# mLSTM gates projected ahead of the HGRN core, and a PSUM bank of its own for the last stream's second norm broadcast

## The chip, the cores and the metric

The kernel runs on one core of a Trainium2 chip. The metric is the device time of one execution in microseconds (us). The core has five engines that matter here: TensorE (PE) for matrix products and transposes, VectorE (DVE), ScalarE (ACT), GpSimd (POOL), and SyncE (SP), which issues most of the DMAs. Each works through its own instructions in program order and waits at semaphores for the others. Products land in PSUM, in banks of 128 partitions by 512 fp32 values; all other tiles lie in SBUF.

## What is computed

Two layers of a trunk over 256 latent tokens and 256 context tokens, model width 1024, batch 1, in fp32. Each layer is a half-step SwiGLU FFN, a mixing of three parallel branches (windowed attention, mLSTM, HGRN2) on one combined projection, and a second half-step FFN. Every one of these sub-layers is wrapped in norms and in a modulation by the condition:

```python
def ada_pre(x, mod, j, g):
    return rms_norm(x, g) * (1.0 + mod[..., 3 * j + 1, :]) + mod[..., 3 * j, :]
def ada_post(x, y, mod, j, g, w):
    return x + w * mod[..., 3 * j + 2, :] * rms_norm(y, g)
def macaron_ffn(x, mod, j, g_pre, g_post, w1, w3, w2):
    h = ada_pre(x, mod, j, g_pre)
    y = (jax.nn.silu(h @ w1) * (h @ w3)) @ w2
    return ada_post(x, y, mod, j, g_post, 0.5)
```

The mLSTM has per token, head (4) and direction (2) an input gate `ml_i` and a log forget gate, `log_sigmoid(m_f + ml_f_bias)`. Their running sums and running maxima along the tokens give the decay between any two tokens and the stabiliser m. The HGRN2 has its own gates, queries and inputs (`h_f`, `h_q`, `h_i`) and does not use those of the mLSTM. Context tokens take part in both layers, but in layer 1 nothing of theirs is needed behind the mixing.

## The kernel before

**Layout.** Activations lie transposed: 128 channels on the partitions, the tokens along the free axis, context stream CS in columns 0 to 255, latent stream XS in 256 to 511. XT is the residual, in eight chunks d of 128 channels. A matrix product keeps fp32 precision by splitting both operands into a rounded high part and the low rest: `mm3` (L255 to L257) does high x high, high x low and low x high into one bank. Weights come in units of 512 rows by 256 columns: one DMA, one cast on ScalarE (`wh`, L238), one subtraction on VectorE (`wl`, L239), 128x1024 each. Input h is split likewise: `Pre.scaled` (VectorE, L389) multiplies a chunk of XT by the norm's broadcast row, ScalarE makes the high half (L397), VectorE the low half (L398).

**Stages.** Layer 0: FFN, mixing, FFN; layer 1: FFN, mixing (latents only behind it), FFN. The five borders that this document calls ends 1 to 5 are: FFN to mixing of layer 0 (around 420 to 446 us of the span), mixing to FFN (1050), FFN of layer 0 to FFN of layer 1 (1440), FFN to mixing of layer 1 (1833), mixing to last FFN (2220). At each of them the end of one stage and the norm ahead of the next are fused in `Post.steps`, stream after stream: first the lead stream (CS), then the last stream (XS). At end 5 there is only XS.

**`Post.steps`.** The stage's sums of squares arrive as columns of a bank. VectorE makes y1, the inverse root for the norm behind the stage (`rsqrt_cols`, L360 to L369, nine operations on 128x2 values), from it by algebra the mean square of the new residual (L512 to L518), and y2, the inverse root for the next norm (the same nine operations). `row_bcast` (L374) turns y1 and then y2 into rows r and r2 by two products each with the identity. VectorE multiplies the eight chunks of the stage's output by r (L530), POOL adds each to XT (L531), and then `Pre.chunk` makes h from XT and r2, chunk by chunk, and the next stage's first products follow. r and r2 share one bank:

```python
                rr = mx()
                r, r2 = rr[:, 0:256], rr[:, 256:512]
```

Three banks rotate in `mx`; a write into a bank waits until its readers are done. The steps are interleaved with the products of the stage by generators (`Pending`, `passes`): while PE works on the lead stream's first products, the last stream's steps run. At end 5 the transposes of XT for the output (L681) also stand in PE's order there.

**Mixing.** `mix` projects HF (the HGRN's forget gates, `passes`), HQ (`proj`, products in L255 to L257) and HI (`proj_tok`, L767 to L769: tokens on the partitions, 24 products of 256 columns to a group, three rotating banks, each group copied out by ScalarE, L770). Then comes the HGRN core (`hgrn`), and behind it the gates of the mLSTM: a DMA of the 16 gate columns on SP (L981), POOL places them in a zeroed 128x1024 tile (L983, L987), ScalarE and VectorE split it (`split_to`, L773, L774), 24 products of 512 columns give the gate values of all tokens (L992 to L994), and a chain follows: Abs, Exp, Ln on ScalarE (L999 to L1001), on VectorE log f (L1002, L1003), three scans for the running sum, cr = i - sum, three scans for the running maximum (L1008 to L1013), the split of cr into crs (cast L773 on ScalarE), lf, and exp(-lf) on ScalarE (L1018, L1019). The projections MQ/MK and MV follow in the code; eight transposes of 64x64 (L1028 running maximum, L1029 exp(-lf)) and two copies put the columns where the heads read them (`mcol`). Each head (`mlstm`) makes decay matrices by products with crs (L1062 to L1065) and Exp on ScalarE (L1071, L1077), multiplies them with q k (L1082 to L1090), normalises, transposes (L1112) and multiplies with v.

**Order.** A scheduler places every engine's instructions from the code; `tc.issue_after(e)` keeps an instruction behind another. So an engine's order is not that of the code, and can be read from the built program only.

Of the kernel before, what the change touches and what calls it, by code (L numbers as in the profile page):

```python
# [10 lines left out]
F32 = mybir.dt.float32  # L11
# [63 lines left out]
def body(tc, I, out, dbg=None):  # L75
    nc = tc.nc
    with tc.tile_pool(name="cst", bufs=1) as cst, \
# [341 lines left out]
        class Post:  # L419
# [82 lines left out]
            def steps(self, st, pre, rest=None):  # L502
# [16 lines left out]
                after = yield  # L519
                rr = mx()  # L520
                r, r2 = rr[:, 0:256], rr[:, 256:512]
# [302 lines left out]
        def mix(l, h, post, need_c, pre):  # L824
# [22 lines left out]
            for b0 in range(2):  # L847
                for u in range(2):
                    us[u] += unit(Win[512 * b0:512 * b0 + 512, OFF_HF + 256 * u:OFF_HF + 256 * u + 256], 4)
                part_end()  # L850
            ps = four()
# [12 lines left out]
            proj(Win, OFF_HQ, 1, h, a, b, cb_hq)  # L864
            proj_tok(Win, OFF_HI, h, HV)

# [111 lines left out]


            graw = tmb((128, 8, 16))  # L980
            nc.sync.dma_start(graw, Win[:, OFF_GATE:OFF_GATE + 16].rearrange("(k p) c -> p k c", p=128))  # L981
            gz, gwh, gwl = slab(shape=(128, 8, 128)), slab(F32R, (128, 8, 128)), slab(F32R, (128, 8, 128))
            G.memset(gz, 0.0)  # L983
            for w in range(2):
                for d in range(2):
                    c0 = 64 * w + 32 * d
                    G.tensor_copy(gz[:, :, c0:c0 + 4], graw[:, :, 8 * w + 4 * d:8 * w + 4 * d + 4])  # L987
            split_to((gwh, gwl), gz)
            gps = bx()
            for k in range(KD):  # L990
                mm(gps, gwh[:, k], h[k][:, 0, :], start=k == 0, stop=False)
                mm(gps, gwh[:, k], h[k][:, 1, :], start=False, stop=False)  # L992
                mm(gps, gwl[:, k], h[k][:, 0, :], start=False, stop=k == KD - 1)
            ip, fp = gps[0:64], gps[64:128]  # L994
# [454 lines left out]
```

## Time and profile before

| | us |
|---|---|
| median of 3 runs | 2432.51 |
| lowest and highest run | 2429.64 and 2435.65 |
| the profiled execution, device time | 2432.19 |
| the profiled execution, span of the trace | 2430.4 |
| PE busy in it | 2366.1 |
| VectorE, ScalarE, POOL busy | 1479.6, 975.5, 240.5 |

The profile comes from one execution. Its page gives busy times, the chain that ended last and the costliest groups of instructions. The trace behind it answers by line, by wait, by window and as a timeline; times there count from the start of the span. In a timeline's row a bracket tells how long the engine was idle ahead of it and what released it. "PEclk" is the clock granted to TensorE as a share of its full 2.4 GHz.

### The profile page before, as it was taken

How to read it: one execution, taken by the hardware profiler on the slowest of the kernel's cores; microseconds unless marked ns; L12 is line 12 of the kernel's file. 1: busy time of each engine (PE TensorE's matmuls, PEld its weight loads, DVE VectorE, ACT ScalarE, POOL GpSimd, SP SyncE). 2: the span in 40 equal slices, each digit the busy share in tenths (PEclk: the TensorE clock that was granted, in tenths of full speed). 3: DMA queues.
4: the chain of work that ended last, by engine and by line, in shares of the span. 5: the costliest groups of instructions: out<-in, count | busy, mean ns of one | idle time of the engine just before them, and what ended most of it. 6: DMA issues, size and time to landing. Idle time of an engine off the chain costs nothing.

```text
span 2430.4 us, 34706 instructions
## 1 busy us (share of the span) xinstructions
PE 2366.1 (97%) x13770; PEld 2004.5 (82%) x13770; DVE 1479.6 (61%) x2677; ACT 975.5 (40%) x1597; POOL 240.5 (10%) x233
## 2 busy tenths in 40 slices
PE   8999999998999999999999999999999989998998
PEld 6877778887887788887778898778799889797998
DVE  5687466655644643767946366874546667656554
ACT  3322332433843732433223332223334374754543
POOL 2000022100000112310002120000221000023000
PEclk9999999999999999999999999999999999998999
DMA  7656343311122033345543325563323125254664
GB/s 262 204 188 199 99 150 101 97 41 36 53 78 87 27 97 94 96 137 194 189 139 100 109 80 197 192 190 106 112 87 89 44 70 145 82 157 120 186 186 135
DMA packets 267270, 301.00 MB, mean 124 GB/s; under 512 B 11709, under 2 KB 233206, under 8 KB 267108
## 3 DMA queue, kind: packets, MB, share of 16 engines
q1 hardware_dynamic: 266448, 298.04, 39.2%
q8 instruction: 108, 1.77, 0.3%
q0 software_dynamic: 512, 0.68, 0.2%
q14 instruction: 54, 0.44, 0.1%
q10 hardware_dynamic: 148, 0.06, 0.0%
HBM read 297.70 MB, written 1.05 MB: 123 GB/s over the span
## 4 chain that ended last, share of the span: by engine, by line
PE 90%; DVE 5%; ACT 3%; issue 1%; DMA 1%; POOL 0%; SPq 0%; DVEq 0%; ACTq 0%; POOLq 0%
PE a L255 24%; PE a L256 24%; PE a L257 24%; PE a L768 1%; PE a L767 1%; PE a L769 1%; PE x L374 1%; PE x L883 1%; PE x L320 1%; PE b L1240 1%; PE x L1300 1%; PE x L1273 1%; PE b L256 1%; PE b L257 1%; PE x L1122 1%
## 5 line engine op out<-in xcount | busy, mean ns | idle before, releaser
L255 PE MATMUL a<-s,wh 128*128 128x512 f32 (+1 forms) x3266 | 1142.3, 351 | 9.1 <-ACT s L397 8.7
L256 PE MATMUL a<-s,wh 128*128 128x512 f32 (+1 forms) x3266 | 1139.6, 349 | 2.2 <-DVE s L398 1.8
L257 PE MATMUL a<-s,wl 128*128 128x512 f32 (+1 forms) x3266 | 1138.2, 349 | 0.0
L239 DVE TENSOR_TENSOR wl<-raw,wh 128x1024 fp32r<-128x1024 f32 (+1 forms) x414 | 515.8, 1256 | 466.5 <-ACT wh L238 461.7
L255 PEld LDWEIGHTS a<-s,wh 128*128 128x128 f32 x3266 | 616.6, 189 | 110.5 <-ACT s L397 10.3
L256 PEld LDWEIGHTS a<-s,wh 128*128 128x128 f32 x3266 | 618.6, 189 | 89.3 <-issue 4.1
L257 PEld LDWEIGHTS a<-s,wl 128*128 128x128 f32 x3266 | 618.3, 189 | 87.0 <-DVE s L615 2.5
L238 ACT CAST wh<-raw 128x1024 fp32r<-128x1024 f32 (+1 forms) x418 | 431.6, 1036 | 608.0 <-PE a L256 422.4
L311 DVE SCALAR_TENSOR_TENSOR s<-s,sc,s 128x512 f32<-128x512 f32 x448 | 306.6, 757 | 0.0
L415 POOL TENSOR_TENSOR s<-s,t 128x512 f32<-128x512 f32 (+1 forms) x35 | 52.3, 1495 | 1074.9 <-ACT s L411 1072.7
L612 DVE TENSOR_TENSOR u<-u,a 128x512 f32<-128x512 f32 (+1 forms) x84 | 51.7, 618 | 101.0 <-PE a L257 98.5
L614 ACT CAST s<-u 128x512 fp32r<-128x512 f32 (+1 forms) x88 | 48.9, 567 | 143.9 <-DVE u L612 126.1
L611 ACT ACTIVATE u<-a 128x512 f32<-128x512 f32 (+1 forms) x88 | 47.4, 542 | 144.4 <-PE a L257 144.4
L767 PE MATMUL a<-wh,s 128*128 128x256 f32 x256 | 74.8, 292 | 7.8 <-ACT s L770 7.3
L397 ACT ACTIVATE s<-t,mod 128x256 fp32r<-128x256 f32 x88 | 38.6, 500 | 94.7 <-DVE t L389 94.7
L1173 POOL TENSOR_TENSOR s<-s,u 128x512 f32<-128x512 f32 (+1 forms) x32 | 35.8, 1119 | 399.0 <-ACT wh L238 253.0
L768 PE MATMUL a<-wl,s 128*128 128x256 f32 x256 | 74.7, 292 | 0.3 <-DVE wl L239 0.3
L769 PE MATMUL a<-wh,s 128*128 128x256 f32 x256 | 74.5, 291 | 0.0
L531 POOL TENSOR_TENSOR XT<-XT,s 128x256 f32<-128x256 f32 x72 | 56.6, 826 | 132.7 <-DVE s L530 58.3
L615 DVE TENSOR_TENSOR s<-u,s 128x512 fp32r<-128x512 f32 (+1 forms) x88 | 53.3, 619 | 15.7 <-ACT s L614 15.5
L767 PEld LDWEIGHTS a<-wh,s 128*128 128x128 f32 x256 | 49.8, 194 | 10.4 <-ACT s L770 9.9
L461 POOL TENSOR_TENSOR s<-s,u 128x512 f32<-128x512 f32 (+1 forms) x29 | 36.9, 1271 | 209.7 <-DVE u L457 199.7
(346 smaller groups left out, 2363.8 us busy)
## 6 DMA issues: line engine op xcount, KB each, us to landing
raw<-in_ffn_w_dram SPq DMA_DIRECT2D x256, 512.0 KB, 3.8
s<-in_w_ada_dram SPq DMA_DIRECT2D x144, 512.0 KB, 6.1
raw<-in_w_in_dram SPq DMA_DIRECT2D x112, 512.0 KB, 3.7
raw<-in_w_out_dram SPq DMA_DIRECT2D x16, 512.0 KB, 3.4
raw<-in_ffn_w_dram SPq DMA_DIRECT2D x16, 256.0 KB, 2.6
raw<-in_w_branch_hg_dram SPq DMA_DIRECT2D x8, 512.0 KB, 3.4
raw<-in_w_branch_ml_dram SPq DMA_DIRECT2D x8, 512.0 KB, 3.4
raw<-in_w_branch_att_dram SPq DMA_DIRECT2D x8, 512.0 KB, 4.1
```

The costliest lines, as they stand in the source:

```text
L238: S.copy(hi[:, :n], raw[:, :n])
L239: (eng or V).tensor_tensor(lo[:, :n], raw[:, :n], hi[:, :n].bitcast(F32), op=ALU.subtract)
L255: mm(ps, hi, h[i][:, 0, a:b], start=first and i == 0, stop=False)
L256: mm(ps, hi, h[i][:, 1, a:b], start=False, stop=False)
L257: end = mm(ps, lo, h[i][:, 0, a:b], start=False, stop=last and i == n - 1)
L311: V.scalar_tensor_tensor(t[:, s], w, c, t[:, s], op0=ALU.mult, op1=ALU.add)
L415: eng.tensor_tensor(dst[:, a:b], dst[:, a:b], q[:, a:b], op=ALU.add)
L531: post_x.append(G.tensor_tensor(xt, xt, yt, op=ALU.add).ins)
L615: V.tensor_tensor(gt[:, 1, a:b], t[:, a:b], gt[:, 0, a:b].bitcast(F32), op=ALU.subtract)
L767: mm(ps, h[k][:, 0, tk], hi, start=k == 0, stop=False)
L768: mm(ps, h[k][:, 0, tk], lo, start=False, stop=False)
L769: mm(ps, h[k][:, 1, tk], hi, start=False, stop=k == KD - 1)
```

## The change

There are two parts. In `mix` the gates move ahead of HGRN: their DMA, the placing on POOL and the split directly behind the weights of HF, the 24 products and the chain behind HQ's projection, the transposes and `mcol` behind HI's projection. In `Post.steps` the last stream's r2 gets a bank of its own; its multiplies and adds are issued four ahead of the second broadcast and two each ahead of chunks 1 and 2; the lead stream's are issued behind its second broadcast; and all multiplies are kept behind the end of y2's chain. The lines of `mix` that are only moved stand once in the diff below; behind the change the lines L530, L531, L767 to L770, L773, L774, L681 have the numbers L533, L534, L782 to L785, L788, L789, L696.

```diff
                 after = yield
+                lead = st is not self.streams[-1]
+
                 rr = mx()
-                r, r2 = rr[:, 0:256], rr[:, 256:512]
+                r = rr[:, 0:256]
                 with tc.issue_after(after) if after is not None else nullcontext():
                     row_bcast(y1, 0, 2, r)
                 y2 = rsqrt_cols(None, 2, None, m)
-                post_x.clear()
-                for d in range(KD):
+                end = tail[0]
+
+                def add(d):
                     yt = self.y(d)[:, lo:hi]
                     xt = XT[:, d, lo:hi]
-                    with tc.issue_after(tail[0]) if st is self.streams[-1] else nullcontext():
+                    with tc.issue_after(end):
                         V.tensor_tensor(yt, yt, r, op=ALU.mult)
                     post_x.append(G.tensor_tensor(xt, xt, yt, op=ALU.add).ins)
+
+                post_x.clear()
+                if not lead:
+                    for d in range(4):
+                        add(d)
                 after = yield
+                r2 = rr[:, 256:512] if lead else mx()[:, 0:256]
                 with tc.issue_after(after) if after is not None else nullcontext():
                     row_bcast(y2, 0, 2, r2)
+                if lead:
+                    for d in range(KD):
+                        add(d)
                 yield
...
                 for d in range(KD):
+                    if not lead and d in (1, 2):
+                        add(2 * d + 2)
+                        add(2 * d + 3)
                     pre.chunk(d, pre.A[:, d, :], st, r2)
...
                 part_end()
+            graw = tmb((128, 8, 16))
+            nc.sync.dma_start(graw, Win[:, OFF_GATE:OFF_GATE + 16].rearrange("(k p) c -> p k c", p=128))
...
+            G.memset(gz, 0.0)
...
+            split_to((gwh, gwl), gz)
             ps = four()
...
             proj(Win, OFF_HQ, 1, h, a, b, cb_hq)
+            gps = bx()
+            for k in range(KD):
+                mm(gps, gwh[:, k], h[k][:, 0, :], start=k == 0, stop=False)
...
+            S.activation(Fc, fp, AF.Abs, bias=fb)
...
+            S.activation(lf, lf, AF.Exp, scale=-1.0)
             proj_tok(Win, OFF_HI, h, HV)
+            pc = mx((128, 2, 4, 64))
...
+            C.free(*grh)
```

How the change moves the instructions is shown at three places.

VectorE at end 1, last stream. In the rows before, L369 is the last link of y2, x_3531 the shared bank of r and r2, L530 the eight multiplies, L389 and L398 the first chunks of h:

```order
L368 TENSOR_TENSOR m_3535<-m_3535,m_3537 128x2
L369 SCALAR_TENSOR_TENSOR m_3534<-m_3535,m_3534 128x2
L530 TENSOR_TENSOR s_2458<-s_2458,x_3531 128x256 x2
L530 TENSOR_TENSOR s_2672<-s_2672,x_3531 128x256 x2
L530 TENSOR_TENSOR s_2899<-s_2899,x_3531 128x256 x2
L530 TENSOR_TENSOR s_3196<-s_3196,x_3531 128x256 x2
L389 SCALAR_TENSOR_TENSOR t_3625<-XT,m_3405,x_3531 128x256
L389 SCALAR_TENSOR_TENSOR t_3629<-XT,m_3405,x_3531 128x256
L389 SCALAR_TENSOR_TENSOR t_3633<-XT,m_3405,x_3531 128x256
L398 SCALAR_TENSOR_TENSOR s_3409<-t_3625,mod_88,s_3409 128x256
```

After, x_3543 is r's bank and x_3603 r2's:

```order
L368 TENSOR_TENSOR m_3547<-m_3547,m_3549 128x2
L369 SCALAR_TENSOR_TENSOR m_3546<-m_3547,m_3546 128x2
L533 TENSOR_TENSOR s_2458<-s_2458,x_3543 128x256 x2
L533 TENSOR_TENSOR s_2672<-s_2672,x_3543 128x256 x2
L389 SCALAR_TENSOR_TENSOR t_3630<-XT,m_3405,x_3603 128x256
L533 TENSOR_TENSOR s_2899<-s_2899,x_3543 128x256 x2
L398 SCALAR_TENSOR_TENSOR s_3409<-t_3630,mod_88,s_3409 128x256
L389 SCALAR_TENSOR_TENSOR t_3638<-XT,m_3405,x_3603 128x256
L533 TENSOR_TENSOR s_3196<-s_3196,x_3543 128x256 x2
L398 SCALAR_TENSOR_TENSOR s_3414<-t_3638,mod_88,s_3414 128x256
```

Four multiplies stand ahead of the first chunk now and two pairs between the first chunks, and L389 reads another bank than the multiplies. Some rows earlier, in the chain of y1 of the same stream, the split of the gate weights (L789; s_3461 is the zeroed tile with the gate columns, s_3462 and s_3463 its high and low half) has come in:

```order
L367 TENSOR_TENSOR m_3495<-m_3494 128x2
L368 TENSOR_TENSOR m_3495<-m_3495,m_3497 128x2
L789 TENSOR_TENSOR s_3463<-s_3461,s_3462 128x1024
L369 SCALAR_TENSOR_TENSOR m_3494<-m_3495,m_3494 128x2
L517 TENSOR_SCALAR m_3510<-m_3509,m_3494 128x1 x2
```

It stands ahead of the last link (L369), and end 4 has the same row at the same place.

ScalarE in the HI projection of layer 0. Before, the second half of HQ (L859, a_3803) is followed by HI's copies (L770, banks a_3845 and on), a scaled copy of the HGRN (L901) and casts of weights (L238):

```order
L859 ACTIVATE u_3828<-a_3803 128x512
L770 COPY s_3382<-a_3845 128x256
L770 COPY s_3382<-a_3871 128x256
L770 COPY s_3383<-a_3897 128x256
L901 COPY s_3392<-s_3378 128x512
L238 CAST wh_4553<-raw_4551 128x1024
L770 COPY s_3383<-a_3923 128x256
```

After, b_3846 is the bank of the gate products, s_3385 and s_3386 the tiles of the chain, s_3883 crs, L885 what L859 was, L785 what L770 was:

```order
L885 ACTIVATE u_3841<-a_3816 128x512
L901 ACTIVATE s_3385<-b_3846,fbias 64x512
L902 ACT_TABLE_LOAD
L902 ACTIVATE s_3385<-s_3385 64x512
L903 ACT_TABLE_LOAD
L903 ACTIVATE s_3385<-s_3385 64x512
L788 CAST s_3883<-s_3386 64x512
L785 COPY s_3382<-a_3900 128x256
L785 COPY s_3382<-a_3926 128x256
L967 COPY s_3386<-s_3378 128x512
L785 COPY s_3383<-a_3952 128x256
L921 ACT_TABLE_LOAD
```

The chain's Abs, Exp, Ln and the cast of cr stand ahead of the first copy of HI now, its last Exp ahead of the fourth.

PE at end 5. Before, L374 makes r and later r2 (both x_18737), L681 transposes XT for the output into banks of its own:

```order
L374 MATMUL x_18737<-cf,m_18712 128x128 x2
L681 MATMUL x_20854<-cf,XT 128x128 x2
L681 MATMUL x_20866<-cf,XT 128x128
L681 MATMUL x_20854<-cf,XT 128x128
L681 MATMUL x_20866<-cf,XT 128x128
L681 MATMUL x_20854<-cf,XT 128x128
L681 MATMUL x_20866<-cf,XT 128x128 x2
L374 MATMUL x_18737<-cf,m_18740 128x128 x2
L255 MATMUL a_18837<-s_18775,wh_18815 128x256
```

After, r2 has x_18765 and L696 is the transposes' line:

```order
L374 MATMUL x_18741<-cf,m_18716 128x128 x2
L374 MATMUL x_18765<-cf,m_18744 128x128 x2
L696 MATMUL x_20859<-cf,XT 128x128 x4
L255 MATMUL a_18842<-s_18772,wh_18820 128x256
L255 MATMUL a_18843<-s_18772,wh_18820 128x256
L255 MATMUL a_18844<-s_18772,wh_18826 128x256
L255 MATMUL b_18845<-s_18772,wh_18826 128x256
L696 MATMUL b_20865<-cf,XT 128x128 x2
```

The second broadcast follows the first directly, and four transposes stand between it and the first product of the FFN (L255), where eight stood ahead of the second broadcast.

In PE's order between the first decay product of the first mLSTM head and its first transpose of weights stand, beside the heads' own small products and the eight transposes of 64x64: before, 24 products of 256 and 42 of 512 columns in layer 0, 120 of 256 columns in layer 1; after, 24 of 512 columns and 27 of 256 columns. On ScalarE four table loads fewer stand in the program.

## Rows read from the trace of the kernel before

**Rows 1.** The page: PE's busy time, and VectorE's 128x1024 subtraction

```profile
PE 2366.1 (97%) x13770; PEld 2004.5 (82%) x13770; DVE 1479.6 (61%) x2677; ACT 975.5 (40%) x1597; POOL 240.5 (10%) x233
...
L239 DVE TENSOR_TENSOR wl<-raw,wh 128x1024 fp32r<-128x1024 f32 (+1 forms) x414 | 515.8, 1256 | 466.5 <-ACT wh L238 461.7
```

**Rows 2.** Waits of PE: line <- releaser, us in total, times, longest

```profile
PE a L255 <- ACT s L397: 8.7, 7, 3.4
PE a L767 <- ACT s L770: 7.3, 8, 2.0
```

**Rows 3.** Windows: stretch, length, busy us (instructions) by engine, PEclk, DMA

```profile
595.50:598.80 3.30, 3.30 (x18) 3.30 (x17) 3.18 (x5) 0.00 (x0) 0.00 (x0) 0.50 0.48 150
...
2217.00:2234.00 17.00, 9.35 (x37) 7.71 (x38) 15.84 (x52) 3.66 (x7) 7.85 (x9) 0.50 0.45 125
```

**Rows 4.** Timeline, PE, end 1: start, us, line, operation [idle before <- releaser]

```profile
421.90 0.71 PE L374 MATMUL x<-cf,m 128*128 128x128 f32 x4 [1.22 <-DVE s L530]
...
442.59 0.71 PE L374 MATMUL x<-cf,m 128*128 128x128 f32 x4 [2.42 <-DVE s L530]
...
444.49 0.62 PE L255 MATMUL a<-s,wh 128*128 128x256 f32 x3 [1.19 <-ACT s L397]
```

**Rows 5.** Timeline, VectorE and POOL at end 1

```profile
432.15 1.27 DVE L398 SCALAR_TENSOR_TENSOR s<-t,mod,s 128x256 fp32r<-128x256 f32 x3
...
439.81 2.73 DVE L530 TENSOR_TENSOR s<-s,x 128x256 f32<-128x256 f32 x8
...
440.30 5.69 POOL L531 TENSOR_TENSOR XT<-XT,s 128x256 f32<-128x256 f32 x8 [16.45 <-DVE s L530]
...
444.60 2.07 DVE L398 SCALAR_TENSOR_TENSOR s<-t,mod,s 128x256 fp32r<-128x256 f32 x3
```

**Rows 6.** Timeline, PE, end 3

```profile
1440.24 0.71 PE L374 MATMUL x<-cf,m 128*128 128x128 f32 x4 [1.35 <-DVE s L530]
...
1442.15 1.01 PE L255 MATMUL a<-s,wh 128*128 128x256 f32 x3 [1.19 <-ACT s L397]
```

**Rows 7.** Timeline, POOL and PE, end 5

```profile
2223.66 6.50 POOL L531 TENSOR_TENSOR XT<-XT,s 128x256 f32<-128x256 f32 x8 [5.30 <-DVE s L530]
...
2224.44 0.48 PE L681 MATMUL x<-cf,XT 128*128 128x128 f32 x1 [3.54 <-POOL XT L531]
...
2229.44 1.01 PE L255 MATMUL a<-s,wh 128*128 128x256 f32 x3 [1.20 <-ACT s L397]
```

**Rows 8.** Timeline, PE around the gate chain, layer 0

```profile
590.09 0.39 PE L767 MATMUL a<-wh,s 128*128 128x256 f32 x1 [1.05 <-ACT s L770]
...
595.17 0.38 PE L767 MATMUL a<-wh,s 128*128 128x256 f32 x1 [1.97 <-ACT s L770]
...
606.18 0.27 PE L1029 MATMUL x<-cf,s 64*128 64x64 f32 x1 [1.20 <-ACT s L1019]
```

**Rows 9.** Timeline, ScalarE and VectorE in the gate chain, layer 0

```profile
590.06 1.28 ACT L1000 ACT_TABLE_LOAD   x1
...
594.23 0.63 ACT L1001 ACTIVATE s<-s 64x512 f32<-64x512 f32 x1
...
598.33 0.69 DVE L1013 TENSOR_TENSOR s<-b,s 64x512 f32<-64x512 f32 x1
```

**Rows 10.** Timeline, PE around the gate chain, layer 1

```profile
1950.80 0.38 PE L767 MATMUL a<-wh,s 128*128 128x256 f32 x1 [1.80 <-ACT s L770]
...
1960.19 0.24 PE L1028 MATMUL x<-cf,s 64*128 64x64 f32 x1 [3.31 <-DVE s L1009]
```

**Rows 11.** Timeline, ScalarE: a copy of the HI projection, layer 0

```profile
475.41 0.37 ACT L770 COPY s<-a 128x256 f32<-128x256 f32 x1 [2.51 <-PE a L769]
```

**Rows 12.** Timeline, ScalarE's last Exp of head 0 and PE's transposes, layer 1

```profile
1980.38 0.63 ACT L1071 ACTIVATE s<-b,mcol 128x128 f32<-128x128 f32 x2
...
1983.74 1.09 PE L1112 MATMUL x<-cf,s 128*128 128x128 f32 x8 [1.00 <-DVE s L1107]
```

**Rows 13.** DMA issues: the gates' columns, count, size each, us to landing

```profile
u<-in_w_in_dram SPq DMA_DIRECT2D x2, 64.0 KB, 3.8
```

More of the change, by code (lines that the diff above doesn't have):

```diff
@@ L850, in mix @@
                 part_end()
+            graw = tmb((128, 8, 16))
+            nc.sync.dma_start(graw, Win[:, OFF_GATE:OFF_GATE + 16].rearrange("(k p) c -> p k c", p=128))
+            gz, gwh, gwl = slab(shape=(128, 8, 128)), slab(F32R, (128, 8, 128)), slab(F32R, (128, 8, 128))
+            G.memset(gz, 0.0)
+            for w in range(2):
+                for d in range(2):
+                    c0 = 64 * w + 32 * d
+                    G.tensor_copy(gz[:, :, c0:c0 + 4], graw[:, :, 8 * w + 4 * d:8 * w + 4 * d + 4])
+            split_to((gwh, gwl), gz)
             ps = four()
@@ L864, in mix, with scans @@
             proj(Win, OFF_HQ, 1, h, a, b, cb_hq)
-            proj_tok(Win, OFF_HI, h, HV)
+            gps = bx()
+            for k in range(KD):
+                mm(gps, gwh[:, k], h[k][:, 0, :], start=k == 0, stop=False)
+                mm(gps, gwh[:, k], h[k][:, 1, :], start=False, stop=False)
+                mm(gps, gwl[:, k], h[k][:, 0, :], start=False, stop=k == KD - 1)
+            ip, fp = gps[0:64], gps[64:128]
+            fb = fbias[64:128, l:l + 1]
+            grh = [C.a4(), C.a4()]
+            lf, Fc = grh[0][0][0:64, 0, :], grh[0][0][0:64, 1, :]
+            cr, Mr = grh[1][0][0:64, 0, :], grh[1][0][0:64, 1, :]
+            S.activation(Fc, fp, AF.Abs, bias=fb)
+            S.activation(Fc, Fc, AF.Exp, scale=-1.0)
+            S.activation(Fc, Fc, AF.Ln, bias=1.0)
+            V.tensor_scalar(lf, fp, fb, 0.0, op0=ALU.add, op1=ALU.min)
+            V.tensor_tensor(lf, lf, Fc, op=ALU.subtract)
+            o32 = ones[0:32, 0:1].to_broadcast([32, 512])
+            o32b = ones[32:64, 0:1].to_broadcast([32, 256])
+            def scans(dst, src, op1):
+                V.tensor_tensor_scan(dst[0:32], o32, src[0:32], 0.0, ALU.mult, op1)
+                V.tensor_tensor_scan(dst[32:64, 255::-1], o32b, src[32:64, 255::-1], 0.0, ALU.mult, op1)
+                V.tensor_tensor_scan(dst[32:64, 511:255:-1], o32b, src[32:64, 511:255:-1], dst[32:64, 0:1], ALU.mult, op1)
+            scans(Fc, lf, ALU.add)
+            V.tensor_tensor(cr, ip, Fc, op=ALU.subtract)
+            scans(Mr, cr, ALU.max)
+            crs = slab(F32R, (128, 512))
+            split_to((crs[0:64], crs[64:128]), cr)
+            V.tensor_tensor(lf, Fc, Mr, op=ALU.add)
+            S.activation(lf, lf, AF.Exp, scale=-1.0)
+            proj_tok(Win, OFF_HI, h, HV)
+            pc = mx((128, 2, 4, 64))
+            for bk in range(4):
+                tk = slice(128 * bk, 128 * bk + 128)
+                nc.tensor.transpose(pc[:, 0, bk, :], Mr[:, tk], ident[0:64, 0:64])
+                nc.tensor.transpose(pc[:, 1, bk, :], lf[:, tk], ident[0:64, 0:64])
+            mcol = smp.tile([128, 2, 4, 2, 4], F32, name=nm("mcol"), tag="mcol", bufs=1)
+            for w in range(2):
+                S.activation(mcol[:, w], cap(pc, 0, 128, 256 * w, [[64, 4], [32, 2], [1, 4]]), AF.Copy, scale=-1.0 if w == 0 else 1.0)
+            C.free(*grh)
             resh = [C.a4(), C.a4()]
@@ L1024, in mix @@
                 proj(Win, OFF_MQ + 256, 1, h, 0, 512, lambda i, ps: cb_mqk(i + 2, ps))
-            pc = mx((128, 2, 4, 64))
-            for bk in range(4):
-                tk = slice(128 * bk, 128 * bk + 128)
-                nc.tensor.transpose(pc[:, 0, bk, :], Mr[:, tk], ident[0:64, 0:64])
-                nc.tensor.transpose(pc[:, 1, bk, :], lf[:, tk], ident[0:64, 0:64])
-            mcol = smp.tile([128, 2, 4, 2, 4], F32, name=nm("mcol"), tag="mcol", bufs=1)
-            for w in range(2):
-                S.activation(mcol[:, w], cap(pc, 0, 128, 256 * w, [[64, 4], [32, 2], [1, 4]]), AF.Copy, scale=-1.0 if w == 0 else 1.0)
-            C.free(*grh)
             MVh = [C.a4(), C.a4()]
```

37 lines of the change are left out of this document (removed).

## The prediction

> **What bounds the kernel now.** I read the page first. TensorE (PE) is busy for 97% of the span [rows 1], so work taken from another engine is worth nothing in itself; a gain must be PE idle time, or PE time at its lower clock. The list of waits says who releases PE: the largest entries are the first product of a block waiting for ScalarE's first half of h (L255 behind L397) and the token-major products waiting for ScalarE's copy out of a bank (L767 behind L770) [rows 2]. The timeline places them: the first sort at ends of stages [rows 4, 6, 7], the second inside the mixing, around the gate chain [rows 8, 10]. Last I read the granted clock by stretches. After such an idle stretch it stands at 0.50, the 1.2 GHz level: from 595.50 PE is busy for all 3.30 us and does what half the time would do at 2.4 GHz, so the stretch costs 1.65 us beside the idle time before it; after the longest idle it is low for 17 us, 9.35 of them busy [rows 3].
>
> **Part 1, the gates moved ahead of HGRN.** Removed: three waits of layer 0, two behind copies that stand on ScalarE among the chain's table loads, 1.05 and 1.97, and 1.20 for the transpose of exp(-lf) [rows 8]: 4.22 us. In layer 1 1.80 and 3.31 [rows 10]: 5.11 us. Together 9.3 us. One half-clock stretch of the 1.65 us kind follows each of the two places; with the idle gone I take both back: 3.3. Sum **12.6 us**. Nothing is saved in instructions but four table loads on ScalarE, which is not the bound.
>
> Added, first: the chain now stands in the window of the HI projection. The order puts Abs, Exp, Ln and the cast of cr on ScalarE ahead of the first two HI copies. From the end of the last gate product: Abs, Exp and Ln, passes over 64x512 at 0.63 each, and two table loads of 1.28, which is 4.45; then from Ln's end (594.86) to the end of cr (599.02) 4.16; then the cast, a pass of the same size, 0.63 [rows 9]; then the first copy, 0.37 [rows 11]: 9.61, say 9.8 with hand-overs. Behind that cast queue the copies, HGRN's first scaled copy and the casts of the next weights. PE needs that copy when it has filled three banks. One group takes 2.51 + 0.37 = 2.88 us [rows 11], three 8.64. PE waits 9.8 - 8.64 = 1.2 us, once, since the later copies find groups already finished. Two layers: **-2.4 us**. If one bank were missing it would be 4.1 each, if ScalarE ran ahead of this estimate nothing; a gain is excluded, since PE did not wait at these copies before. The chain's last Exp and the eight transposes stand a whole projection later and wait for nothing. VectorE, which now scans in that window, has little else queued there. On SP the gates' DMA moves ahead of the loads of HQ and HI, 64 KB that land in 3.8 us [rows 13], for weights that PE reads behind a whole pass: nothing. On POOL the memset and copies now stand between the adds of the two streams at ends 1 and 4 (below).
>
> Added, second: what lay behind the chain as cover is gone. The first mLSTM head needs decay matrices from ScalarE, and before it the order now leaves little else for PE: in layer 1 27 products of 256 columns (0.12 each, a 24th of 2.88) between the first decay matmul and the transposes of the weights, where 120 stood, with 28 small ones of the heads (22 such widths): 5.9 us. The head's chain is a table load 1.28, eight Exps at 0.32 to 0.5 (two of the small ones took 0.63), and from the last Exp (1981.01) to the transposes 2.73 [rows 9, 12]: 6.6 to 8.0. PE waits 0.7 to 2.1 there; it waited 1.00 at that place before too, under a slower ScalarE. Layer 0 has twice the Exps (9.1 to 12.0 us against 24 products of 0.24 and the small ones, 24 such widths, 8.7): 0.4 to 3.3. I take 1.6 and 1.9: **-3.5 us**, bounds 0 and -6.
>
> Added, third: at ends 1 and 4 the split of the gate weights now stands on VectorE inside the chain of y1, ahead of its last link, and everything at the end is queued behind it: y1's broadcast, y2, the multiplies, the first h. It is a 128x1024 subtraction, 1.26 us [rows 1]. Its partner on ScalarE follows the last square of the stage, and POOL's memset and copies follow the lead stream's eight adds; both are done before VectorE is there. It is charged below.
>
> **Part 2, ends of stages.** Last stream, end 1: the broadcast of y2 waits until VectorE has read r out of the shared bank eight times, 439.81 to 442.54, and comes at 442.59; the first product follows at 444.49, 1.19 us after the broadcast's end [rows 4, 5]. With a bank of its own the broadcast runs under the multiplies; four of them end at 441.18, 1.19 us later the products start: 442.37, a gain of 2.1. At end 3 the same pair of waits stands (1.35, 1.19) [rows 6]: 2.1. End 4 repeats it. At ends 1 and 4 the split takes 1.26 of it: 0.85 each. End 2 has PE covered by the other stream: 0. At end 5 the output's transposes of X stood between the broadcasts and waited for POOL's adds, 3.54, and the first product came at 2229.44 [rows 7]. Now the second broadcast stands ahead of them, but four transposes still stand ahead of the first product, and need POOL's fourth add: 2223.66 + 4 x 0.81 = 2226.9, product at some 2227.1; of these 2.3 us 0.5 goes to transposes pushed behind it: 1.8. Last streams: 2.1 + 2.1 - 2 x 1.26 + 2.1 + 1.8 = 5.6.
>
> Lead stream, end 1: multiplies no longer stand between the links of y2's chain, PE's wait of 1.22 goes [rows 4]; what is late next is POOL, whose adds start some 4 us later and then lie beside the lead's L398. That price shows at the last stream: three L398, two of them beside POOL's adds (which end at 445.99), took 2.07, against 1.27 for three without [rows 5]: 0.4 more for each of the two. Two of them reach PE: 1.2 - 0.8 = 0.4. In the last streams all of the first L398 now stand beside the adds, which already hit one or two of them: 0.4 at each of four ends, -1.6. The half clock after end 3 should go, since its idle falls from 2.5 us to under 1: 1.65; at the other ends I leave it. Part 2: 5.6 + 0.4 - 1.6 + 1.65 = **6.0 us**.
>
> The Trainium skill speaks harder on this, in "SBUF — State Buffer", section "SBUF: two separate sides": GpSimd and a VectorE operation with two SBUF inputs take one port pair in turn, and the loser is blocked for the winner's whole instruction. L398 and POOL's add are such a pair. By that rule the sum would be rival F's. The rows lie between: 0.4 more, not 0.71.
>
> **Sum.** 12.6 - 2.4 - 3.5 + 6.0 = 12.7 us, against the profiled execution's 2432.19 (0.3 below the median of 2432.51): **2419.5 us**, -0.5%.
>
> **Rivals.**
> (B) ScalarE becomes the bound in both windows. For: the order gives it the whole chain without a copy between. HI's waits then each drop the clock (2 x 1.65), the first heads take their upper bound (2.5 more) and drop it too (2 x 1.65): 9.1 us worse, 2428.6. Against: the idle stretches would be about 1 to 2 us, and PE waited 1.22 at 421.90 without a stretch of low clock among those I found.
> (C) The ends give nothing: POOL's adds, 5.69 us for eight [rows 5], pace the first h, or the new bank has a late reader and the broadcast waits as before. 2425.5. Against: the adds run 0.71 apart, and a block's h is used only every 12 products of 0.12.
> (E) Better: no wait at the first heads (3.5), the clock kept at ends 1 and 4 too (3.3), no loss by L398 (2.4): 2410.3. For: ScalarE has four table loads fewer.
> (F) Each of the first two L398 waits out a whole 0.71 us add of POOL at each of the four last-stream ends: 1.42 instead of 0.4, 1.0 more per end, 2423.5. Against: 0.4 is what two of them lost [rows 5].
> (D) Slower. The split in y1's chain needs ScalarE's cast, that POOL's copies, those the 64 KB of gate weights, whose buffer a sum on POOL held before. If that buffer came free only with the stage's last sums, landing (3.8 [rows 13]) and a cast as long as the split (1.26 [rows 1]) would put the split 5.1 us late at ends 1 and 4, 10.2 us, and an idle of that size brings the long low clock, half of 9.35 each [rows 3]: 19.5 us worse, 2439. It decides from (12.7 - 9.35) / 2 = 1.7 us of lateness on. Against: POOL was idle for 16.45 us ahead of the last stream's adds [rows 5], so its sums were long done.
>
> **How the numbers follow.** Forecast 0.44, B 0.14, C 0.11, E 0.17, F 0.08, D 0.06. The range takes in the forecast with its bounds, C, F, B and the near half of E: 2409 to 2429. A measurement tells about 0.3%, 7.3 us, from no change, so faster is below 2425.2: 0.41 of the forecast, E, F, half of C and a little of B, 0.72; within: the rest of B and C, D up to 2439.8 and a forecast that falls short, 0.23; slower 0.05.
>
> **What would show it.** Right: no PE wait among the token-major products ahead of the first head's decay, one wait of about 1.2 us at the fourth HI group in each layer, a broadcast of y2 directly behind its chain, and a clock of 1.00 after end 3. Wrong: a wait of more than 3 us at HI or at the first head; the split ending later than 1.3 us behind the link ahead of it; ends of the last stream where PE idles as long as in [rows 4, 6]; new stretches at 0.50.

## The result and the profile after

The changed kernel takes 2413.15 us (median of 4 runs, 2410.74 to 2416.82) where the kernel before takes 2434.08 beside it: ratio 0.9914, 95% interval 0.9898 to 0.9931. Beside later experiments it was timed again at 2416.66, ratio 0.9932 (0.9915 to 0.9948). So it is faster by 0.7 to 0.9%, some 16 to 21 us, and lies inside the predicted range, nearer its middle than its lower end in the second series. The profiled execution took 2410.74, with a span of 2409.0 against 2430.4.

First the page's busy line and the largest entries of the list of waits of the changed kernel:

```profile
PE 2356.6 (98%) x13770; PEld 1999.4 (83%) x13770; DVE 1469.2 (61%) x2677; ACT 970.4 (40%) x1593; POOL 242.4 (10%) x233
```

```profile
PE x L374 <- DVE m L369: 11.2, 8, 5.4
...
PE a L255 <- ACT s L397: 10.0, 7, 1.9
...
PE a L782 <- ACT s L785: 4.3, 6, 1.2
```

Against [rows 1, 2]: PE is busy for 9.5 us less. The copies of the token-major products (L785 now) release PE after 4.3 us of waiting instead of 7.3, and the largest of these waits is the 1.23 of the HI projection, described below. The first products of blocks still wait for L397, 10.0 us against 8.7: this entry grew.

The timeline of PE at end 1 (lead, then last stream) and at end 3 (lead, then last), to be laid beside [rows 4, 6]:

```profile
424.59 0.62 PE L255 MATMUL a<-s,wh 128*128 128x256 f32 x3 [1.24 <-ACT s L397]
...
438.57 0.68 PE L374 MATMUL x<-cf,m 128*128 128x128 f32 x4 [0.87 <-DVE m L369]
...
440.73 1.01 PE L255 MATMUL a<-s,wh 128*128 128x256 f32 x3 [1.48 <-ACT s L397]
```

```profile
1417.07 1.01 PE L255 MATMUL a<-s,wh 128*128 128x256 f32 x3 [1.27 <-ACT s L397]
...
1433.60 0.62 PE L255 MATMUL a<-s,wh 128*128 128x256 f32 x3 [1.36 <-ACT s L397]
```

The second broadcast (L374) is no longer released by the multiplies but by its own chain, and in the last streams 3.61 us of waiting became 2.35 at end 1, 2.54 became 1.36 at end 3. The lead streams lost: L255 waits 1.24 and 1.27 where it had waited 0.29 and not at all, and at end 3 the 0.53 for L398 is gone into it. Behind the lead stream's first wait at ends 2, 3 and 4 (0.90, 1.27 and 1.28) the clock falls, in the windows (columns as in [rows 3]):

```profile
1024.30:1027.70 3.40, 3.40 (x18) 3.40 (x17) 3.27 (x6) 1.30 (x4) 2.38 (x3) 0.51 0.00 0
...
1417.00:1420.40 3.40, 3.33 (x16) 3.33 (x17) 3.35 (x6) 1.49 (x5) 0.30 (x1) 0.51 0.00 0
...
1809.40:1812.80 3.40, 3.40 (x18) 3.40 (x18) 3.40 (x6) 1.01 (x3) 3.34 (x5) 0.51 0.00 0
```

Each is the first block of a lead stream. In the kernel before, the low stretch of end 3 lay at the last stream.

Where the time went is told by stretches between starts of PE's sums of squares (L490): the last stream's at ends 1, 3 and 4, the lead's at end 2, the only ones at end 5. The first row counts from the start of the span, the last row ends with the start of PE's last product. In us:

| stretch | before | gates alone | ends alone | changed | lead as before | the last version |
|---|---|---|---|---|---|---|
| start to end 1 | 418.3 | 416.6 | 418.7 | 416.6 | 417.7 | 418.7 |
| end 1 and first mixing | 591.9 | 587.8 | 587.9 | 582.2 | 582.8 | 581.3 |
| end 2 and second FFN | 407.7 | 407.6 | 411.2 | 410.2 | 406.4 | 406.7 |
| end 3 and third FFN | 393.0 | 393.3 | 391.8 | 391.9 | 389.3 | 389.8 |
| end 4 and second mixing | 397.6 | 387.4 | 397.4 | 388.1 | 384.0 | 381.5 |
| end 5 and last FFN | 214.8 | 215.3 | 211.8 | 212.9 | 212.2 | 212.7 |

The columns behind the first are the profiled executions of e1, e2, the changed kernel, e10 and e11 below. The first row has nothing of the change in it: 1.7 us of its difference stand by 16 us after the start, where the transposes of the input (L218) go four in 0.85 us until 14.79 in the kernel before, and four in 0.44 to 0.59 us from 10.85 on in the changed one. Of the other 19.7 us the two mixings hold 9.7 and 9.5; end 5 gains 1.9, end 3 1.1, and end 2 loses 2.5.

### The profile page after: what moved, and what is told of

Read it like the earlier page. It is cut to its first block, busy times and chain, and to the rows that moved or that the text cites. A ratio compares the mean times of both kernels' runs of the same rounds, so it can differ in the third digit from the quotient of the medians.

```text
span 2409.0 us, 34700 instructions
## 1 busy us (share of the span) xinstructions
PE 2356.6 (98%) x13770; PEld 1999.4 (83%) x13770; DVE 1469.2 (61%) x2677; ACT 970.4 (40%) x1593; POOL 242.4 (10%) x233
## 4 chain that ended last, share of the span: by engine, by line
PE 92%; DVE 3%; ACT 3%; issue 1%; POOL 0%; DMA 0%; SPq 0%; DVEq 0%; ACTq 0%; POOLq 0%
PE a L255 25%; PE a L256 25%; PE a L257 25%; PE a L782 1%; PE a L784 1%; PE a L783 1%; PE x L949 1%; PE x L320 1%; PE x L374 1%; PE b L256 1%; PE b L255 1%; PE x L1315 1%; PE b L257 1%; PE b L1255 1%; PE x L1288 1%
## 5 line engine op out<-in xcount | busy, mean ns | idle before, releaser
L255 PE MATMUL a<-s,wh 128*128 128x512 f32 (+1 forms) x3266 | 1140.0, 351 | 10.0 <-ACT s L397 10.0
L255 PEld LDWEIGHTS a<-s,wh 128*128 128x128 f32 x3266 | 616.0, 189 | 109.6 <-ACT s L397 11.0
L238 ACT CAST wh<-raw 128x1024 fp32r<-128x1024 f32 (+1 forms) x418 | 431.3, 1034 | 613.6 <-PE a L256 430.1
L782 PE MATMUL a<-wh,s 128*128 128x256 f32 x256 | 73.3, 286 | 4.3 <-ACT s L785 4.3
L397 ACT ACTIVATE s<-t,mod 128x256 fp32r<-128x256 f32 x88 | 39.5, 501 | 93.2 <-DVE t L389 93.2
L534 POOL TENSOR_TENSOR XT<-XT,s 128x256 f32<-128x256 f32 x72 | 53.0, 774 | 139.9 <-DVE s L533 139.9
L446 ACT ACTIVATE s<-a,R 128x256 f32<-128x256 f32 x77 | 34.0, 471 | 52.9 <-PE a L257 48.8
```

What stands on the lines that cost most here:

```text
L238: S.copy(hi[:, :n], raw[:, :n])
L255: mm(ps, hi, h[i][:, 0, a:b], start=first and i == 0, stop=False)
L782: mm(ps, h[k][:, 0, tk], hi, start=k == 0, stop=False)
```

## Experiments

e3, e4 and e7 to e10 were executed once each; the others are medians of 4 to 6 runs.

**e1 and e2: each part alone.** e1 takes the moved gates and leaves `Post.steps` as it was; e2 the reverse.

e1, against the changed kernel:

```diff
-                r = rr[:, 0:256]
+                r, r2 = rr[:, 0:256], rr[:, 256:512]
...
+                for d in range(KD):
...
+                    with tc.issue_after(tail[0]) if st is self.streams[-1] else nullcontext():
...
-                if not lead:
-                    for d in range(4):
-                        add(d)
...
-                r2 = rr[:, 256:512] if lead else mx()[:, 0:256]
```

e2, against the changed kernel, with the rest of the gates' chain moved likewise:

```diff
-            split_to((gwh, gwl), gz)
             ps = four()
...
             proj(Win, OFF_HQ, 1, h, a, b, cb_hq)
-            gps = bx()
...
             proj_tok(Win, OFF_HI, h, HV)
-            pc = mx((128, 2, 4, 64))
...
+            split_to((gwh, gwl), gz)
+            gps = bx()
...
             if need_c:
...
                 proj(Win, OFF_MQ + 256, 1, h, 0, 512, lambda i, ps: cb_mqk(i + 2, ps))
+            pc = mx((128, 2, 4, 64))
```

> Only the mixing's part of the change; ends of stages as before. Theory P, the terms of the prediction (gates 12.6, HI -2.4, first heads -3.5, split -2.5): 4.2 us below before's span of 2430.4, 2426. Theory R, read from the changed kernel's trace (no wait at the first heads, HI wait of 1.23 each, two half-clock stretches gone): some 15 us, a span near 2415, with the wait at the fourth HI group still 1.2 and none above 0.5 at the first head.

> Only the part at the ends of stages; gates where they were. Theory P: 8.5 us (6.0 and the split's 2.5, which this kernel does not pay), a span of 2422. Theory R: the last streams gain as forecast, but the lead streams of ends 1, 3 and 4 lose, since ScalarE casts a second weight ahead of the first L397: about 4 us, a span near 2426, with waits of 1.2 us of L255 for L397 at the lead streams of ends 3 and 4 that were 0.5 before, and half-clock stretches behind them.

e1: median 2421.39, ratio 0.9943 (0.9927 to 0.9960), span 2415.0. e2: 2426.90, ratio 0.9968 (0.9955 to 0.9980), span 2425.8. Both spans are where theory R had put them. By the stretches behind the first row the gates alone give 13.7 us and the ends alone 4.9; together 19.7. By the medians it is 13.4 and 7.9. So the mixing's part brings most of it, and the forecast had it the other way round (4.2 and 8.5). In e1 the price of the split is bare, since the end around it is still the old one; PE at end 1, to be laid beside [rows 4]:

```profile
441.96 1.23 PE L374 MATMUL x<-cf,m 128*128 128x128 f32 x4 [3.42 <-DVE s L530]
```

3.42 against 2.42: 1.00 of the split's 1.26.

**e3: the split of cr behind the HI projection.**

```diff
-            crs = slab(F32R, (128, 512))
-            split_to((crs[0:64], crs[64:128]), cr)
...
             proj_tok(Win, OFF_HI, h, HV)
+            crs = slab(F32R, (128, 512))
+            split_to((crs[0:64], crs[64:128]), cr)
```

> The changed kernel with the split of cr (cast on ScalarE, subtraction on VectorE) in the code behind the HI projection, so that ScalarE's first two HI copies stand behind Ln only. If the wait at the fourth HI group comes from the cast waiting for cr: the copy is done some 4.9 us after the last gate product, under 8.64, the wait of 1.23 goes in both layers, span 2409.0 - 2.5 = 2406.5. If it comes from the table loads or the banks: the wait stays at 1 us or more, span 2408 to 2409.

2414.61, span 2412.8. In the changed kernel the timelines of ScalarE and PE in the HI projection of layer 0 read:

```profile
470.59 0.69 ACT L901 ACTIVATE s<-b,fbias 64x512 f32<-64x512 f32 x1 [1.64 <-PE b L895]
...
474.54 0.63 ACT L903 ACTIVATE s<-s 64x512 f32<-64x512 f32 x1
...
479.35 0.62 ACT L788 CAST s<-s 64x512 fp32r<-64x512 f32 x1 [4.18 <-DVE s L915]
...
480.00 0.65 ACT L785 COPY s<-a 128x256 f32<-128x256 f32 x2
```

```profile
480.42 0.39 PE L782 MATMUL a<-wh,s 128*128 128x256 f32 x1 [1.23 <-ACT s L785]
```

Ln ends at 475.17; ScalarE then stands idle for 4.18 us at the cast of cr (L788), with two finished groups of HI behind it, and PE waits 1.23 at the fourth. In e3 the first copy follows Ln directly:

```profile
477.27 0.63 ACT L903 ACTIVATE s<-s 64x512 f32<-64x512 f32 x1
...
477.93 0.38 ACT L785 COPY s<-a 128x256 f32<-128x256 f32 x1
```

and PE has no wait among these products in either layer; its idle time in the two mixings fell by 1.4 and 1.3 us. The span did not show that: the start took 2.7 us more, and low-clock stretches stood at places where the first profile of the changed kernel had none. e5 was made for that.

**e4, e10, e12: the lead stream.** e4 gives the lead its own bank for r2, and all eight multiplies behind y2's chain but ahead of the second broadcast in the code. e10 puts the lead back to what it was.

e10, against the changed kernel:

```diff
-                    with tc.issue_after(end):
+                    with tc.issue_after(end) if not lead else nullcontext():
...
-                if not lead:
-                    for d in range(4):
-                        add(d)
+                for d in range(KD if lead else 4):
+                    add(d)
...
-                if lead:
-                    for d in range(KD):
-                        add(d)
```

e4 has the second and third of these pieces, and

```diff
-                r2 = rr[:, 256:512] if lead else mx()[:, 0:256]
+                r2 = mx()[:, 0:256]
```

> The changed kernel with the lead stream treated like the last one: own bank for r2, all eight multiplies directly behind y2's chain and ahead of the second broadcast in the code. If the lead's waits of 0.9 to 1.28 at ends 1 to 4 come from multiplies and weight casts that the late issue let in ahead of the first h: these waits fall below 0.6 and the three half-clock stretches at 1024, 1417 and 1809 us go, 3 to 4 us of idle and 5 of clock, span 2401 to 2403. If ScalarE's casts stand ahead of L397 either way: 2408 to 2410.

> The changed kernel with the lead stream as in the kernel before (shared bank, eight multiplies between the links of y2's chain, adds early); the last stream as changed. If the late multiplies are the lead's loss: PE's waits of 1.27 at the lead of ends 3 and 4 fall back to 0.53 without half clock behind them, end 1 gets its 1.22 back at the broadcast instead of 1.24 at the first product, and the stretch from the last stream of end 2 on is as long as before, some 2.5 us less than in the changed kernel. If not: 1.2 and more stays at ends 3 and 4.

> The kernel with the lead stream as before and nothing else undone, timed this time. Its profile was 9.5 us shorter than the changed kernel's; if that is the lead's issue order and the four or five half-clock stretches it brought, the median stands near 2403, 0.4 to 0.6% below the changed kernel's (2413 to 2417) and 1.2% below before. If that one profile was a lucky one: 2410 or more.

e4: 2406.73, span 2405.0, between its two expectations: the first waits of the leads at ends 3 and 4 fell to 0.33 and 0.34, but 0.79 for L398 (VectorE's low halves) came behind each, and 0.87 for L397 stayed at end 2. e10: 2401.24, span 2399.5. e12, the same kernel timed: 2403.94 (2401.67 to 2404.60), ratio 0.9874 (0.9858 to 0.9891). So the lead's part of the change costs 9 to 13 us by the medians, and the kernel is better without it. The reason is in ScalarE's order. The changed kernel at the lead stream of end 3, ScalarE and the VectorE row that it should have followed:

```profile
1414.26 1.99 ACT L238 CAST wh<-raw 128x1024 fp32r<-128x1024 f32 x2 [1.43 <-PE b L256]
...
1416.15 0.47 ACT L446 ACTIVATE s<-a,R 128x256 f32<-128x256 f32 x1
...
1416.52 1.70 ACT L397 ACTIVATE s<-t,mod 128x256 fp32r<-128x256 f32 x4
```

```profile
1414.23 1.65 DVE L389 SCALAR_TENSOR_TENSOR t<-XT,m,x 128x256 f32<-128x256 f32 x4
```

The first scaled chunk (L389) is done by 1414.65, but L397 starts at 1416.52: two casts of weights, 1.99 us, and L446 stand ahead of it. In e10:

```profile
1412.04 0.47 ACT L446 ACTIVATE s<-a,R 128x256 f32<-128x256 f32 x1 [1.18 <-DVE s L468]
...
1412.41 1.04 ACT L238 CAST wh<-raw 128x1024 fp32r<-128x1024 f32 x1
...
1413.35 1.70 ACT L397 ACTIVATE s<-t,mod 128x256 fp32r<-128x256 f32 x4
```

```profile
1415.19 0.39 PE L256 MATMUL a<-s,wh 128*128 128x256 f32 x1 [0.54 <-DVE s L398]
...
1428.91 0.62 PE L255 MATMUL a<-s,wh 128*128 128x256 f32 x3 [0.17 <-ACT s L397]
```

One cast stands ahead of L397, the other behind it, and PE waits 0.54, as before. With the lead on time the last stream's wait at end 3 goes almost wholly: 0.17 here, 1.36 in the changed kernel, 2.54 before. And the clock, in the windows of e10:

```profile
546.50:2188.00 1641.50, 1625.42 (x9296) 1367.41 (x9294) 996.86 (x1867) 686.86 (x1172) 178.69 (x165) 1.00 0.37 113
```

1.00 from 546 us to the start of end 5: no low stretch at ends 2, 3 and 4 at all. In e12, the same program, one of 3.4 us stood at end 1 and one at end 2.

**e5: the changed kernel again.**

> The changed kernel itself once more, beside the others of this call. If the runs of 2411 and of 2416 us of the same program differ by the number of half-clock stretches and by the first 30 us (DMA) alone: idle between 30 us and the end within 0.5 us of the first profile's, every wait above 0.8 us at the same place, and from the end of the first half-clock stretch to the start of the last one 2379 us as in the first profile, plus 1.7 for each stretch of 3.4 more. If the schedule itself drifts: waits at other places.

2416.66 (2414.31 to 2418.11); the profile has a span of 2415.3. Its waits above 0.8 us stand where they stood, idle time in each of the five later stretches is within 0.5 us of the first profile's. The difference is the start (2.5 us) and the clock. The windows of the first profile, then of this one:

```profile
541.00:549.00 8.00, 8.00 (x50) 7.14 (x50) 4.03 (x13) 1.96 (x4) 0.00 (x0) 1.00 0.23 66
```

```profile
542.80:549.60 6.80, 6.80 (x20) 5.04 (x19) 3.35 (x17) 1.63 (x2) 0.00 (x0) 0.50 0.04 3
...
1027.50:1034.30 6.80, 6.52 (x29) 6.23 (x30) 4.94 (x11) 2.71 (x7) 2.38 (x3) 0.50 0.01 2
```

The same products of the HGRN's stretch ran at 1.00 in one execution and for 6.80 us at 0.50 in the other, and the low stretch at end 2 lasted 6.80 instead of 3.40. So two spans of one program differ by 6.3 us here, and for less than that the stretches and the waits have to be compared one by one.

**e7: the split of the gate weights behind y2's chain.**

```diff
-            split_to((gwh, gwl), gz)
...
             passes([(ps[i], us[i // 2], 128 * (i % 2)) for i in range(4)], h, [CS, XS])
+            with tc.issue_after(tail[0]):
+                split_to((gwh, gwl), gz)
```

> The changed kernel with one edit: the split of the gate weights (VectorE, 128x1024) kept behind y2's chain of the last stream instead of inside y1's. If it costs its full length there: the two waits at the last stream of ends 1 and 4 (0.87 and 1.48) fall by 1.2 us together, to some 1.1, 2.5 us in all. If ScalarE or POOL was the later one anyway: the two waits stay within 0.3 of 2.35.

2409.44, span 2407.7. PE at the last streams of ends 1 and 4:

```profile
441.62 0.63 PE L255 MATMUL a<-s,wh 128*128 128x256 f32 x3 [1.25 <-ACT s L397]
...
1827.28 0.62 PE L255 MATMUL a<-s,wh 128*128 128x256 f32 x3 [1.24 <-ACT s L397]
```

One wait of 1.25 instead of 0.87 and 1.48, at both: 1.10 each. The split was on the path with nearly its full length.

**e8: two more table loads at the first head.**

```diff
+                    if hd == 0 and d == 0:
+                        S.activation(small((128, 1)), Dt[2][:, 0, 0:1], AF.Ln, bias=1.0)
```

> The changed kernel with a one-column Ln on ScalarE between the first head's Exps of direction 0 and those of direction 1, which brings two more table loads, 2.6 us and the Ln itself. It tells how much slack the first head's chain has. If PE's own products there only just cover the chain (8.7 us against 8.7 in layer 1): PE waits 2.5 us or more ahead of the first transposes of weights in layer 1. If ScalarE has a spare of several us since the chain left: under 1 us.

2423.09, span 2421.3. PE at the first head in layer 0 and in layer 1:

```profile
610.27 0.49 PE L1077 MATMUL b<-s,idr 128*128 128x512 f32 x1 [2.35 <-ACT s L1092]
...
1966.07 0.58 PE L1077 MATMUL b<-s,idr 128*128 128x256 f32 x1 [2.73 <-ACT s L1086]
```

Of 2.76 us added to ScalarE, 2.35 and 2.73 reach PE. The wait stands at the next decay products, which need a bank, not at the transposes. In the changed kernel the same place has no wait, so the cover is just long enough: 0.4 us are spare in layer 0, next to nothing in layer 1.

**e9: r2 back in the shared bank, the rest as changed.**

```diff
-                r2 = rr[:, 256:512] if lead else mx()[:, 0:256]
+                r2 = rr[:, 256:512]
```

> The changed kernel with the last stream's r2 back in r's bank; order of the multiplies as in the change. If the bank matters by itself: the second broadcast waits for the four multiplies that read r (1.37 us) and the first h for the broadcast (0.71), so that y2 to first product takes 2.3 + 0.7 to 0.9 = 3.1 us at end 3 and the idle there rises from 1.36 to 2.1 or more, likewise 0.7 to 0.9 at ends 1, 4 and 5. If POOL's first add and the order of the multiplies are what paces the first h: no more than 0.2 at each end.

2425.52, span 2423.8. PE, second broadcasts of the last streams of ends 1 and 3:

```profile
441.67 0.71 PE L374 MATMUL x<-cf,m 128*128 128x128 f32 x4 [2.10 <-DVE s L533]
...
1440.69 0.71 PE L374 MATMUL x<-cf,m 128*128 128x128 f32 x4 [1.15 <-DVE s L533]
```

With 1.19 behind each for L397 this is 3.29 against 2.35 at end 1 and 2.34 against 1.36 at end 3; end 4 has 3.31. So the bank itself is worth 0.94 to 0.98 us of idle an end, and the last stretch, end 5, is 2.3 us longer without it. By this one execution the time without the bank is 9 to 12 us above the changed kernel's medians, the clock included. The rest goes with the new order of the multiplies: with the bank shared, the two waits are 1.32 shorter than in e1 at end 1 and 0.20 shorter than before at end 3. No run has the own bank with the old order. Low stretches in the row of the first mixing were 13.7 us, against 3.4 in the changed kernel and 10.2 in its repetition (e5), so not all of that belongs to the longer waits.

**e6 and e11: three edits together.** Both have e3's and e7's edits; e6 has e4's lead, e11 e10's.

> The changed kernel with three edits: the lead's multiplies first and an own bank (worth 7 from end to end of the clock's first and last stretch, where it was tried alone), the cr split behind HI (two waits of 1.23), and the split of the gate weights kept behind y2's chain at ends 1 and 4. If the split costs its 1.26 at both ends and the three add: 2379.1 - 7 - 2.5 - 2.5 = 2367 between those stretches, a span near 2399. If the split was hidden or only moves the wait to the gate products: 2370 and 2402 or more.

> The changed kernel with the lead stream as before, the split of the gate weights behind y2's chain, and the cr split behind HI. If the three edits add as each did alone by stretch: the stretch of end 1 and the first mixing 582.2 - 1.1 - 1.2 = 580, the second FFN 406.4, the third 389.3, end 4 with the second mixing 384.0 - 1.1 - 1.2 = 381.7, all without half clock but one near 540; a span near 2394, 1.5% below before. If the waits that go let the next ones grow, as the split's place did at end 3's idle: 2397 to 2400.

e6: 2401.33 (2398.16 to 2405.15), ratio 0.9871 (0.9857 to 0.9886). e11: 2399.13 (2398.43 to 2400.31), ratio 0.9857 (0.9843 to 0.9872), span 2397.8. By the stretches the three add up to within 1.3 us each (last column of the table), though the span is 3.8 us above the 2394 of that expectation. At end 1 one wait is left in the last stream:

```profile
442.58 0.63 PE L255 MATMUL a<-s,wh 128*128 128x256 f32 x3 [1.25 <-ACT s L397]
```

e11 beats both kernels, by 1.4% the one before and by 0.6 to 0.7% the changed one.

## Why the prediction was right, step by step

The forecast was 12.7 us, and 16 to 21 came. Direction and range were right, and several terms to a few hundredths. That the sum came out so near is in part luck: the gates brought 9.5 us more than forecast (13.7 instead of 4.2) and the ends 3.6 less (4.9 instead of 8.5), and the errors partly cancel.

- **The waits of the gate chain** (9.3) and the two low stretches behind them (3.3): gone, in e1 and in the changed kernel, at both layers.
- **HI, 1.2 us in each layer:** 1.23 and 1.23. The sum over the chain against three groups of 2.88 was right in its parts, and e3 shows the link that decides: the cast that waits for cr.
- **The first heads, -3.5:** this step failed; the term was 0. The chain's length was read about right (6.6 to 8.0 us; 8.15 from the table load at 1951.89 to the transposes at 1960.04, with a cast of some 1 us among it), the cover wrong. I had priced the small products of the heads by their columns, 2.64 us for all. PE at the first head of layer 1, and ScalarE's chain beside it:

```profile
1951.30 0.28 PE L1077 MATMUL b<-s,idr 128*128 128x256 f32 x1
...
1951.92 0.48 PE L1097 MATMUL x<-s,s 64*128 64x128 f32 x2
...
1953.56 0.38 PE L1099 MATMUL x<-s,s 64*128 64x128 f32 x2
...
1953.87 0.39 PE L255 MATMUL a<-s,wh 128*128 128x256 f32 x1
...
1960.04 1.09 PE L1127 MATMUL x<-cf,s 128*128 128x128 f32 x8
```

```profile
1951.89 1.28 ACT L1086 ACT_TABLE_LOAD   x1
...
1956.43 0.52 ACT L1092 ACTIVATE s<-b,mcol 128x256 f32<-128x256 f32 x1
```

From 1951.30 to the transposes at 1960.04 the timeline has 27 products of h, which with the pauses between them fill 3.79 us where I had 3.24, and 34 small ones (I had counted 28), which fill 4.95 from start to start. The twelve with 64 rows (L1097 to L1099) stand between 1951.92 and 1953.87: 1.95 us, where their columns (eight widths of 256 at 0.12) make 0.96. So the cover is 8.74 us instead of 5.9, as long as the chain, and e8 shows that hardly anything is spare. Left out of the sum besides: the wait of 1.00 at this head before, and 0.96 behind it by the same timeline, which went as well.
- **Gates in all:** forecast 4.2 with the split, measured 13.7 (e1). The first heads explain 3.5, the two waits just named 2.0, smaller waits about 1. Some 3 us are left. Part of them is that a wait costs PE more than its bracket says. In the kernel before, to be laid around the wait of 1.80 at 1950.80 [rows 10]:

```profile
1948.72 0.28 PE L769 MATMUL a<-wh,s 128*128 128x256 f32 x1
...
1951.03 0.28 PE L768 MATMUL a<-wl,s 128*128 128x256 f32 x1
```

From 1948.72 to 1951.03 pass 2.31 us for two products that take 0.24 in a stream: 2.07 lost, 0.27 more than the bracket. Counted like this, the seven waits that went (five of the chain, two at the first head of layer 1) cost 1.7 us beyond their brackets, and the two that came at HI 0.5. That is 1.2 of the 3 us; the rest stays open.
- **The split, 1.26 at two ends:** 1.10 (e7).
- **The last streams, 2.1 from the bank and the order:** at end 3 from the end of y2's chain to the first product 4.6 us became 2.3. Only half of it became less idle, since the lead was late; in e10 all of it did. End 5, forecast 1.8, has 1.95: the second broadcast at 2203.93, the first product at 2207.15, with four transposes between that wait for POOL's adds, as worked out.

```profile
2203.93 1.19 PE L374 MATMUL x<-cf,m 128*128 128x128 f32 x4 [2.50 <-DVE m L369]
...
2207.15 0.99 PE L255 MATMUL a<-s,wh 128*128 128x256 f32 x3
```

- **The lead stream, +0.4:** this step failed in its sign. The wait of 1.22 at end 1 went and one of 1.24 came in its place; ends 2, 3 and 4, which I had put at nothing, lost 0.5 to 0.8 each at the first wait and a low stretch; new stretches at 0.50 had been among the signs of being wrong. I had followed VectorE and POOL, where the multiplies were moved, and not ScalarE, where the later first chunk let a second cast pass ahead of L397. The lead's part of the change costs 9 to 13 us (e12).
- **L398 beside POOL's adds, 0.4 each:** too much. VectorE at the last stream of end 3, and the adds of POOL that were running when these began:

```profile
1433.58 0.49 DVE L398 SCALAR_TENSOR_TENSOR s<-t,mod,s 128x256 fp32r<-128x256 f32 x1
...
1435.05 0.60 DVE L398 SCALAR_TENSOR_TENSOR s<-t,mod,s 128x256 fp32r<-128x256 f32 x1
...
1437.14 0.95 DVE L398 SCALAR_TENSOR_TENSOR s<-t,mod,s 128x256 fp32r<-128x256 f32 x1
```

```profile
1433.06 0.73 POOL L534 TENSOR_TENSOR XT<-XT,s 128x256 f32<-128x256 f32 x1
...
1434.63 0.74 POOL L534 TENSOR_TENSOR XT<-XT,s 128x256 f32<-128x256 f32 x1
...
1436.90 0.91 POOL L534 TENSOR_TENSOR XT<-XT,s 128x256 f32<-128x256 f32 x1
```

A single L398 past the last add takes 0.48 (at 1439.59). These three take 0.01, 0.12 and 0.47 more, and each ends 0.28 or 0.29 us after its add (1433.79, 1435.37 and 1437.81). So what is lost is what is left of the add, which can be nearly nothing, and the 0.4 of the forecast was two cases with much left. At the last streams of ends 1, 3 and 4 PE waits for no L398. Rival F, the whole add of 0.71 each time, fell. The Trainium skill's rule in "SBUF — State Buffer", "SBUF: two separate sides", is that whichever of the two operations starts first holds the shared port pair for its whole instruction, while the other is blocked. These rows agree with it: a blocked L398 loses the rest of the add and not the whole of it, so rival F is not what the rule gives.
- **The clock after end 3, 1.65:** the low stretch left the last stream and came back at the lead (1417.00). Net nothing; in e10, where both waits are small, it is gone.
- **Rivals.** B fell (no wait at the heads, no low clock at HI), C fell (e9), D fell (the split waited for nobody). E, the better case, was the nearest in its mechanism: no wait at the heads, no wait of PE for L398 in those last streams. Its kept clock at ends 1 and 4 did not come (low for 3.4 us at 440.7 and at 1826.5).

## What to carry to other kernels

Where an edit delays a step, read the new order on every engine that feeds the next step, also on those where nothing was moved: here ScalarE's weight casts slipped ahead of the first h and cost more than the edit's own gain at that place. A chain that is moved away from its cover needs its new cover priced from rows of the same small instructions, not by the columns. And two waits in a row, here one for a bank and one for the first h behind it, are worth pricing together: with the own bank, the new order of the multiplies and the lead on time, 2.54 us became 0.17 at end 3, and the low stretch behind them went as well (e10).

## What was not expected of the hardware

The granted clock of the same program at the same place differed between executions: the HGRN products at 541 to 549 us ran at 1.00 in one profile and for 6.80 us at 0.50 in another, with the same waits ahead of them, and the clock and the start together make 6 us of 2410. It could also be kept: with the lead stream back (e10) it stayed at 1.00 for 1641 us, over three ends where lead waits of 0.9 to 1.3 us had each been followed by a low stretch in the changed kernel. There these waits were 0.43 to 0.54; but 1.12 for L397 at the last stream of end 4 brought none, and the same program had low stretches at ends 1 and 2 in e12. And the small products of the heads took twice the time of their columns: twelve with 64 rows fill 1.95 us in the rows above, 0.22 for one of 256 columns and mostly 0.11 for one of 128, from start to start, where a product of 256 columns in a long stream takes 0.12.
